# Rotary embedding: the first tile loaded in pieces of 1, 3 and 4 rows, tables behind the first row, and other rows and PSUM buffers

## The chip, the cores and the metric

One core of a Trainium2 chip. The experiments were spread over three chips: e1 to e4 and e9 to e12 ran on one, e5 to e8 on another, e13 to e15 on a third; every ratio is to runs of before in the same rounds on the same chip. The metric is device microseconds (us) of one execution; a kernel's time is the median of its fast runs. Beside it stands the span of the profiled execution, which is 1.8 to 1.9 us shorter.

## The reference

```python
batch, seq, dim = 16, 512, 1024          # float32, 16 heads of 64, half = 32
x = x.reshape(batch, seq, 16, 64)
x1, x2 = x[..., :32], x[..., 32:]        # cos, sin: (512, 32)
out = concatenate([x1*cos - x2*sin, x1*sin + x2*cos], axis=-1)
```

33.6 MB are read and 33.6 MB written; each element takes two products and a sum.

## The kernel before

The 16 x 512 positions are eight tiles (4 MiB each) of 128 partitions by eight rows of 1024 elements. A partition's eight rows lie together in HBM, so a tile is 128 runs of 32 KB. Five tiles have a buffer.

```python
BUFS = 5
PE_ROWS = (0, 2, 4, 6)
DVE_B = ((0,), (0, 4))
FIRST = (3, 8)                 # the first tile: rows 0-2, then 3-7
...
    pe = ctx.enter_context(tc.tile_pool(name="pe", bufs=2, space=bass.MemoryType.PSUM))
    pd = ctx.enter_context(tc.tile_pool(name="pd", bufs=1, space=bass.MemoryType.PSUM))
...
    load(0, 0, FIRST[0])                                  # all loads and stores: SyncE's queue
    for sb, v, parts in ((sin_sb, sin_v, SIN_PARTS), (cos_sb, cos_v, COS_PARTS)):
        ...  nc.sync.dma_start(out=sb[lo:hi, :], in_=v[lo:hi, :])
    for lo, hi in zip(FIRST, FIRST[1:]):
        load(0, lo, hi)
    for t in range(1, BUFS):
        load(t)
...  # the tables are spread to 128 partitions by two matmuls
    for t in range(NT):
        for k in range(KK):
            ...
            if not own:       # own: k in DVE_B[t % 2]
                nc.gpsimd.tensor_tensor(out=halves(b), in0=swapped(r, nh), in1=over_heads(sk), op=ALU.mult)
            if k in PE_ROWS:  # PSUM += by TensorE, ScalarE copies back
                ps = pe.tile([P, dim], FP32, name="ps")
                nc.vector.tensor_tensor(out=pairs(ps), in0=pairs(r), in1=cos_b(k), op=ALU.mult)
                ...           # two matmuls with the identity add the sine part
                nc.scalar.copy(out=r, in_=ps)
            else:             # VectorE adds, one row later
                nc.vector.tensor_tensor(out=pairs(ps), in0=pairs(r), in1=cos_b(k), op=ALU.mult)
                pending.append((r, ps, b))
        ...
        store(t)              # the last tile in two halves
        if t + 1 == NT - BUFS:
            for n in range(BUFS, NT):
                load(n)       # each waits for the store that frees its buffer
```

## Time and profile before

163.27 us (median of 3, 163.15 to 163.57), span 161.6 us.

| what | value | where |
|---|---|---|
| bytes moved, rate 3 to 158 us | 67.28 MB, 430 GB/s | page; windows of time |
| DMA queue's share of 16 engines' span | 97.5% | page, part 3 |
| VectorE, GpSimd busy | 128.9, 121.0 us | page, part 1 |
| VectorE's first row product, last add's end | 10.96, 142.96 us | timeline |
| least time from a store's issue to its landing | 17.5 us | view of out_dram |

Lines of the page of before. The second line is part 1. The DMA line gives the busy tenths of the DMA engines in 40 slices of the span, the GB/s line what they moved. The queue line is part 3, the next the chain of work that ended last, the last four the DMA issues with size and time from issue to landing.

```profile
span 161.6 us, 692 instructions
...
PE 81.8 (51%) x136; PEld 30.3 (19%) x136; DVE 128.9 (80%) x115; ACT 33.7 (21%) x33; POOL 121.0 (75%) x58
...
DMA  5999999999999999999999999999999999999992
GB/s 189 395 441 435 454 454 389 446 462 389 438 470 389 389 446 464 389 454 446 397 454 446 397 448 446 406 454 438 406 450 438 406 448 438 414 454 389 438 426 118
...
q1 hardware_dynamic: 2752, 67.24, 97.5%
...
DVE 37%; PE 18%; issue 17%; POOL 6%; ACT 4%; DMA 4%; SPq 0%; DVEq 0%; ACTq 0%; POOLq 0%
...
xt<-in_x_dram SPq DMA_DIRECT2D x1, 2560.0 KB, 11.3
xt<-in_x_dram SPq DMA_DIRECT2D x1, 1536.0 KB, 6.2
b<-in_sin_dram SPq DMA_DIRECT2D x1, 64.0 KB, 6.3
b<-in_cos_dram SPq DMA_DIRECT2D x1, 64.0 KB, 6.1
```

The DMA is full from the second slice to the last but one, so the bytes set the time. The chain of waits names VectorE first, yet it ends with the last store's issue at 143 us, and the transfers go on for 17 us more.

Windows of time of before: the last two columns are the DMA engines' busy share and GB/s. In such a window a DMA packet counts with all its bytes where it starts, so short windows are ragged.

```profile
3.00:4.00 1.00, 0.08 (x1) 0.00 (x0) 0.00 (x0) 0.00 (x0) 0.00 (x0) 1.00 0.99 418
4.00:5.00 1.00, 0.00 (x0) 0.00 (x0) 0.00 (x0) 0.00 (x0) 0.00 (x0) 1.00 1.00 418
5.00:6.00 1.00, 0.00 (x0) 0.00 (x0) 0.00 (x0) 0.00 (x0) 0.00 (x0) 1.00 0.96 406
...
143.00:158.00 15.00, 0.00 (x0) 0.00 (x0) 0.00 (x0) 0.00 (x0) 0.00 (x0) 0.58 0.98 422
```

The head flows at 406 to 418 GB/s; after 143 us, with all compute engines idle, the rate (422 GB/s) is close to the 430 of the whole stretch from 3 to 158 us.

SyncE's timeline of before: start and duration of each DMA issue (not of the transfer).

```profile
0.73 0.38 SPq L75 DMA_DIRECT2D xt<-in_x_dram  x1
1.17 0.53 SPq L87 DMA_DIRECT2D b<-in_sin_dram  x1
1.75 0.58 SPq L87 DMA_DIRECT2D b<-in_cos_dram  x1
2.37 2.65 SPq L75 DMA_DIRECT2D xt<-in_x_dram  x5
28.04 0.35 SPq L79 DMA_DIRECT2D out_dram<-xt  x1
```

### The profile page before, as it was taken

The page shows a single profiled execution, that of the slowest core. Times are in us where ns is not written, and L with a number is a line of the kernel's source. Part 1 is how long each engine was busy: PE and PEld are TensorE (multiplying, and loading weights), DVE is VectorE, ACT ScalarE, POOL GpSimd, SP SyncE. Part 2 cuts the span into 40 slices and gives each one's busy share as a digit, 9 for nine tenths or more (in the row PEclk, how much of TensorE's full clock was granted, in tenths as well). Part 3 has the DMA queues.
Part 4 walks back from the last instruction along what each step waited for, and adds up shares of the span by engine and source line. Part 5 has one row for each costly group of instructions (what it writes and reads, how often), then busy time and mean ns, then how long its engine had stood idle before and what let it go on. Part 6 is the DMA issues. An engine that isn't in the chain of part 4 may idle for free.

```text
span 161.6 us, 692 instructions
## 1 busy us (share of the span) xinstructions
PE 81.8 (51%) x136; PEld 30.3 (19%) x136; DVE 128.9 (80%) x115; ACT 33.7 (21%) x33; POOL 121.0 (75%) x58
## 2 busy tenths in 40 slices
PE   4136946496429742955097419660984194600000
PEld 1112301241114211311032114210321131100000
DVE  1059897999999989999999999999999999930000
ACT  0003242023302430223113302222223122220000
POOL 1049999999999999999994199999999997000000
PEclk9999996559975998799969965999689879995555
DMA  5999999999999999999999999999999999999992
GB/s 189 395 441 435 454 454 389 446 462 389 438 470 389 389 446 464 389 454 446 397 454 446 397 448 446 406 454 438 406 450 438 406 448 438 414 454 389 438 426 118
DMA packets 2756, 67.28 MB, mean 416 GB/s; under 512 B 320, under 2 KB 448, under 8 KB 448
## 3 DMA queue, kind: packets, MB, share of 16 engines
q1 hardware_dynamic: 2752, 67.24, 97.5%
q8 instruction: 1, 0.02, 0.0%
q14 instruction: 3, 0.02, 0.0%
HBM read 33.69 MB, written 33.55 MB: 416 GB/s over the span
## 4 chain that ended last, share of the span: by engine, by line
DVE 37%; PE 18%; issue 17%; POOL 6%; ACT 4%; DMA 4%; SPq 0%; DVEq 0%; ACTq 0%; POOLq 0%
PE ps L168 17%; DVE xt L150 12%; DVE pd L178 12%; DVE ps L163 7%; POOL b L160 6%; DVE xt L165 5%; ACT xt L171 4%; DMA b<-in_sin_dram 4%; PE tab L110 1%; PE tab L111 1%; DVE tab L118 0%; DVE sns L113 0%; SPq L75 0%; DVE sns L114 0%; DVEq L150 0%
## 5 line engine op out<-in xcount | busy, mean ns | idle before, releaser
L160 POOL TENSOR_TENSOR b<-xt,sns 128x1024 f32<-128x1024 f32 x52 | 120.3, 2350 | 14.5 <-DVE sns L114 9.2
L168 PE MATMUL ps<-xt,ident 128*128 128x512 f32 x48 | 35.8, 888 | 39.2 <-issue 24.5
L171 ACT COPY xt<-ps 128x1024 f32<-128x1024 f32 x32 | 32.4, 1012 | 95.2 <-PE ps L168 90.8
L168 PE MATMUL ps<-b,ident 128*128 128x512 f32 x80 | 43.5, 674 | 14.7 <-DVE ps L163 12.1
L150 DVE TENSOR_TENSOR xt<-pd,b 128x1024 f32<-128x1024 f32 x32 | 39.0, 1218 | 2.2 <-POOL b L160 1.1
L163 DVE TENSOR_TENSOR ps<-xt,tab 128x1024 f32<-128x1024 f32 x32 | 39.1, 1223 | 1.5 <-ACT xt L171 1.3
L178 DVE TENSOR_TENSOR pd<-xt,tab 128x1024 f32<-128x1024 f32 x32 | 39.3, 1227 | 0.8
L168 PEld LDWEIGHTS ps<-b,ident 128*128 128x128 f32 x80 | 17.1, 227 | 44.1 <-issue 30.6
L168 PEld LDWEIGHTS ps<-xt,ident 128*128 128x128 f32 x48 | 11.6, 267 | 58.8 <-issue 46.1
L165 DVE TENSOR_TENSOR xt<-xt,tab 128x1024 f32<-128x1024 f32 x12 | 14.6, 1220 | 0.4
L113 DVE TENSOR_SCALAR sns<-tab 128x256 f32<-128x256 f32 x1 | 0.4, 425 | 8.0 <-PE tab L111 8.0
L171 ACT ACT_TABLE_LOAD x1 | 1.3, 1283 | 13.5 <-DVE xt L165 13.5
L110 PE MATMUL tab<-b,spread 64*128 64x256 f32 x2 | 1.2, 697 | 4.5 <-DMA b<-in_sin_dram 4.5
L101 PE MATMUL ps<-zero 128*128 128x512 bf16 x4 | 1.9, 625 | 1.2 <-DVE zero L97 1.2
L110 PEld LDWEIGHTS tab<-b,spread 64*128 64x128 f32 x2 | 0.5, 308 | 5.4 <-issue 5.4
L111 PE MATMUL tab<-b,spread 64*128 64x256 f32 x2 | 1.1, 631 | 0.0
L97 DVE MEMSET zero<- 128x256 uint32 x1 | 0.3, 272 | 0.9 <-PEq L208 0.9
L101 PEld LDWEIGHTS <-zero 128*128 128x128 bf16 x4 | 0.4, 129 | 1.7 <-DVE zero L97 1.2
L111 PEld LDWEIGHTS tab<-b,spread 64*128 64x128 f32 x2 | 0.7, 333 | 0.2
L118 DVE COPY tab<-sns 128x64 f32<-128x64 f32 x2 | 0.5, 228 | 0.1
L109 DVE COPY spread<-ident 64x64 f32<-64x64 f32 x2 | 0.3, 182 | 0.2 <-POOL ident masks.py:199 0.2
masks.py:197 POOL MEMSET ident<- 128x128 f32 x1 | 0.2, 204 | 0.3 <-POOLq L208 0.3
(6 smaller groups left out, 1.1 us busy)
## 6 DMA issues: line engine op xcount, KB each, us to landing
xt<-in_x_dram SPq DMA_DIRECT2D x7, 4096.0 KB, 29.5
out_dram<-xt SPq DMA_DIRECT2D x7, 4096.0 KB, 30.3
out_dram<-xt SPq DMA_DIRECT2D x2, 2048.0 KB, 18.1
xt<-in_x_dram SPq DMA_DIRECT2D x1, 2560.0 KB, 11.3
xt<-in_x_dram SPq DMA_DIRECT2D x1, 1536.0 KB, 6.2
b<-in_sin_dram SPq DMA_DIRECT2D x1, 64.0 KB, 6.3
b<-in_cos_dram SPq DMA_DIRECT2D x1, 64.0 KB, 6.1
```

What stands on the lines that cost most here:

```text
L101: nc.tensor.matmul(out=ps[:, c : c + BANK], lhsT=zero[:, :P], rhs=zero, start=True, stop=True)
L110: nc.tensor.matmul(out=sin_t, lhsT=spread, rhs=sin_sb, start=True, stop=True)
L111: nc.tensor.matmul(out=cos_t, lhsT=spread, rhs=cos_sb, start=True, stop=True)
L113: nc.vector.tensor_scalar_mul(out=sns[:, :, 0, :], in0=sin_k, scalar1=-1.0)
L118: nc.vector.tensor_copy(out=sns_t[:, i * hd : (i + 1) * hd], in_=sns[:, k])
L150: nc.vector.tensor_tensor(out=r, in0=ps, in1=b, op=ALU.add)
L160: nc.gpsimd.tensor_tensor(out=halves(b), in0=swapped(r, nh), in1=over_heads(sk), op=ALU.mult)
L163: nc.vector.tensor_tensor(out=pairs(ps), in0=pairs(r), in1=cos_b(k), op=ALU.mult)
L165: nc.vector.tensor_tensor(out=halves(r), in0=halves(r), in1=swapped_signed(k), op=ALU.mult)
L168: nc.tensor.matmul(out=ps[:, c : c + BANK], lhsT=ident, rhs=rhs, start=False, stop=True, skip_group_check=True)
L171: nc.scalar.copy(out=r, in_=ps)
L178: nc.vector.tensor_tensor(out=pairs(ps), in0=pairs(r), in1=cos_b(k), op=ALU.mult)
```

## The change

Its intent: start the compute earlier (one row and the tables suffice), let TensorE, ScalarE and VectorE wait less for PSUM (three single-bank buffers and two of two banks in place of two and one of two banks), and keep adds one row behind. The core of the diff:

```diff
-PE_ROWS = (0, 2, 4, 6)
-DVE_B = ((0,), (0, 4))
-FIRST = (3, 8)
+PE_ROWS = (0, 3, 6)
+DVE_B = ((0,), (0,))
+FIRST = (1, 4, 8)
...
-    pe = ...(name="pe", bufs=2, ...)      # tiles of 1024 (two banks)
-    pd = ...(name="pd", bufs=1, ...)
+    pe = ...(name="pe", bufs=3, ...)      # tiles of 512 (one bank)
+    pd = ...(name="pd", bufs=2, ...)
...
-                ps = pe.tile([P, dim], FP32, name="ps")
-                nc.vector.tensor_tensor(out=pairs(ps), in0=pairs(r), in1=cos_b(k), op=ALU.mult)
+                for c in range(0, dim, BANK):
+                    ps = pe.tile([P, BANK], FP32, name="ps")
+                    nc.vector.tensor_tensor(out=pairs(ps), in0=pairs(rc), in1=cos_b(k, BANK // half), op=ALU.mult)
...   # matmul and ScalarE's copy also by halves; at most one add pending
+            if k == 0 and t > 0:
+                finish(t - 1)             # last add and store of the tile before
```

More of the change, by code (lines that the diff above doesn't have):

```diff
@@ L16 @@
 BANK = 512
-PE_ROWS = (0, 2, 4, 6)
-DVE_B = ((0,), (0, 4))
-FIRST = (3, 8)
+PE_ROWS = (0, 3, 6)
+DVE_B = ((0,), (0,))
+FIRST = (1, 4, 8)
 LAST_OUT = (4, 8)
-SIN_PARTS = (64,)
-COS_PARTS = (64,)
 @with_exitstack
@@ L63 @@
     pfix = ctx.enter_context(tc.tile_pool(name="pfix", bufs=1, space=bass.MemoryType.PSUM))
-    pe = ctx.enter_context(tc.tile_pool(name="pe", bufs=2, space=bass.MemoryType.PSUM))
-    pd = ctx.enter_context(tc.tile_pool(name="pd", bufs=1, space=bass.MemoryType.PSUM))
+    pe = ctx.enter_context(tc.tile_pool(name="pe", bufs=3, space=bass.MemoryType.PSUM))
+    pd = ctx.enter_context(tc.tile_pool(name="pd", bufs=2, space=bass.MemoryType.PSUM))
     ctx.enter_context(tc.manual_schedule())
@@ L83 @@
     cos_sb = bp.tile([P, dim], FP32, name="b")[:PB, : KK * half]
-    for sb, v, parts in ((sin_sb, sin_v, SIN_PARTS), (cos_sb, cos_v, COS_PARTS)):
-        lo = 0
-        for hi in parts:
-            nc.sync.dma_start(out=sb[lo:hi, :], in_=v[lo:hi, :])
-            lo = hi
+    nc.sync.dma_start(out=sin_sb, in_=sin_v)
+    nc.sync.dma_start(out=cos_sb, in_=cos_v)
     for lo, hi in zip(FIRST, FIRST[1:]):
@@ L97 @@
     nc.vector.memset(zero, 0.0)
-    for i in range(2):
-        ps = pe.tile([P, dim], FP32, name="ps")
-        for c in range(0, dim, BANK):
-            nc.tensor.matmul(out=ps[:, c : c + BANK], lhsT=zero[:, :P], rhs=zero, start=True, stop=True)
+    for i in range(3):
+        ps = pe.tile([P, BANK], FP32, name="ps")
+        nc.tensor.matmul(out=ps, lhsT=zero[:, :P], rhs=zero, start=True, stop=True)
     sns = fixed.tile([P, KK, 2, half], FP32)
@@ L118, with cos_b @@
         nc.vector.tensor_copy(out=sns_t[:, i * hd : (i + 1) * hd], in_=sns[:, k])
-    def cos_b(k):
+    def cos_b(k, n):
         c = cos_t[:, k * half : (k + 1) * half]
-        return bass.AP(tensor=c.tensor, offset=c.offset, ap=[c.ap[0], [0, 2 * nh], [1, half]])
+        return bass.AP(tensor=c.tensor, offset=c.offset, ap=[c.ap[0], [0, n], [1, half]])
     def over_heads(s):
@@ L146, with add, finish @@
     pending = []
-    def add():
-        r, ps, b = pending.pop(0)
-        nc.vector.tensor_tensor(out=r, in0=ps, in1=b, op=ALU.add)
+    def add(most):
+        while len(pending) > most:
+            r, ps, b = pending.pop(0)
+            nc.vector.tensor_tensor(out=r, in0=ps, in1=b, op=ALU.add)
+    def finish(t):
+        add(0)
+        lo = 0
+        for hi in LAST_OUT if t == NT - 1 else (KK,):
+            store(t, lo, hi)
+            lo = hi
+        if t + 1 == NT - BUFS:
+            for n in range(BUFS, NT):
+                load(n)
     for t in range(NT):
@@ L161 @@
             if k in PE_ROWS:
-                ps = pe.tile([P, dim], FP32, name="ps")
-                nc.vector.tensor_tensor(out=pairs(ps), in0=pairs(r), in1=cos_b(k), op=ALU.mult)
+                parts = []
+                for c in range(0, dim, BANK):
+                    ps = pe.tile([P, BANK], FP32, name="ps")
+                    rc = r[:, c : c + BANK]
+                    nc.vector.tensor_tensor(
+                        out=pairs(ps), in0=pairs(rc), in1=cos_b(k, BANK // half), op=ALU.mult
+                    )
+                    parts.append((ps, rc, swapped(rc, BANK // hd) if own else b[:, c : c + BANK]))
                 if own:
                     nc.vector.tensor_tensor(out=halves(r), in0=halves(r), in1=swapped_signed(k), op=ALU.mult)
-                for c in range(0, dim, BANK):
-                    rhs = swapped(r[:, c : c + BANK], BANK // hd) if own else b[:, c : c + BANK]
-                    nc.tensor.matmul(
-                        out=ps[:, c : c + BANK], lhsT=ident, rhs=rhs, start=False, stop=True, skip_group_check=True
-                    )
-                nc.scalar.copy(out=r, in_=ps)
-                while pending:
-                    add()
-            else:
-                while pending:
-                    add()
+                for ps, rc, rhs in parts:
+                    nc.tensor.matmul(out=ps, lhsT=ident, rhs=rhs, start=False, stop=True, skip_group_check=True)
+                    nc.scalar.copy(out=rc, in_=ps)
+            else:
+                add(1)
                 ps = pd.tile([P, dim], FP32, name="pd")
-                nc.vector.tensor_tensor(out=pairs(ps), in0=pairs(r), in1=cos_b(k), op=ALU.mult)
+                nc.vector.tensor_tensor(out=pairs(ps), in0=pairs(r), in1=cos_b(k, 2 * nh), op=ALU.mult)
                 pending.append((r, ps, b))
-        while pending:
-            add()
-        if t < NT - 1:
-            store(t)
-        else:
-            lo = 0
-            for hi in LAST_OUT:
-                store(t, lo, hi)
-                lo = hi
-        if t + 1 == NT - BUFS:
-            for n in range(BUFS, NT):
-                load(n)
+            if k == 0 and t > 0:
+                finish(t - 1)
+            add(1)
+    finish(NT - 1)
 _INS = ['x', 'cos', 'sin', 'num_heads']
```

## The prediction

> **What bounds the kernel now: the DMA engines.** The page counts 67.28 MB moved and a DMA strip that reads 9 in every slice from the second to the last but one. By windows of time, 3 to 158 us moved 430 GB/s at a DMA share of 1.00. The Trainium skill, "DMA: Bandwidth & Descriptors", section "Specifications", puts the fabric ceiling at 435 GB/s; this trace agrees. The rate does not depend on the compute: 143 to 158 us, with every compute engine idle, moved 422 GB/s.
>
> The chain of waits names DVE 37% and PE 18%, but it ends at 142.96 us, when the last store is issued; that lands 17.5 us later (least issue-to-landing among stores). So compute runs well ahead. The second half of the last store (2.1 MB, about 4.9 us at 430 GB/s) can first move at about 154 us: some 11 us to spare.
>
> **What the change does.**
> - *Head.* 0.5 MB instead of 1.57 MB lies before the tables, so they land about 2.5 us earlier (1.05 MB at 418 GB/s): near 5 us, not 7.43; DVE's first row product starts near 8.4 us, not 10.96. But the same 20 MB of loads queue, and the first store waits behind them (issued 28.04, loads run to about 52).  Cost: one more DMA and 128 packets; perhaps 0 to 0.3 us of bubble while the short first piece drains.
> - *DVE.* Rows through PE go from 32 to 24, so 8 more rows take a second DVE pass (add, 1.218 us); rows with DVE's own product go from 12 to 8 (1.220 us each saved); 24 products split into 48 of 512. From 1.222 us for 1024 and 0.24 us for 64 elements I estimate 0.69 us a half. Sum about +8 us: DVE busy near 138 us, not 128.9.
> - *POOL.* 56 instead of 52 products at 2.35 us: about 131 us, +9.
> - *ACT* 48 copies of 512 (about 0.55 us each, estimate): about 26 us. *PE*: 96 recorded main matmuls instead of 128.
> - *PSUM.* Three single banks for PE rows and two pairs for DVE rows, adds deferred by one: fewer waits between DVE, ACT and POOL. Stores are issued one row later, about 3 us. All off the critical path.
>
> Compute should end at 145 to 152 us (8.4 + 138 + a few us of waits), still before the queue runs dry at about 154. The DMA then finishes where it did.
>
> **Predicted: 163.3 us**, 162.6 to 164.4 holding 8 times in 10. Chances: faster by over 2%: 0.02; within 2%: 0.94; slower by over 2%: 0.04. The Trainium skill, "Perfetto Trace Analysis", section "DMA Optimizations", says splitting DMAs may pay when the engines are generally idle; here they are not.
>
> **What would show each step.** Right: DMA strip still at 9, about 430 GB/s in the middle, span within 1 us of 161.6; DVE starts near 8.4 us, is busy near 138 us, ends 145 to 152; POOL about 131 us; last store's issue to landing falls to about 10 us, yet time stays. Wrong: a hole in the DMA strip near 3 us or after 140 us, or a different rate with equal bytes.
>
> **What would make it wrong.** Compute ending after about 153 us (slow clock stretching PE, POOL late), each us then costing one; a lower DMA rate from the smaller head pieces or another overlap of loads and stores; or a start bubble over 0.3 us.

## The result, and the profile after

| | before | after |
|---|---|---|
| time, median of 6 runs each | 163.32 us (163.13 to 163.57) | 164.97 us (164.42 to 165.42) |
| ratio of fast runs | | 1.0098 (1.0077 to 1.0120) |
| span of the profiled run | 161.6 us | 163.0 us |

A ratio here is the mean time of one kernel's fast runs over that of the other's fast runs of the same rounds, so it is not quite the ratio of the medians. The outputs are right. The change is about 1% slower: within the 2% that counts as the same, but clear of noise and outside the predicted range.

The lines of the page of after that answer to those of before:

```profile
span 163.0 us, 616 instructions
...
PE 78.3 (48%) x103; PEld 24.8 (15%) x103; DVE 131.8 (81%) x142; ACT 29.4 (18%) x49; POOL 130.2 (80%) x62
...
DMA  5999999999999999999999999999999899999992
GB/s 153 348 435 470 418 442 442 402 450 450 418 442 306 452 434 426 450 410 442 442 410 442 450 396 466 426 434 442 410 434 466 386 442 458 410 450 394 438 418 92
...
q1 hardware_dynamic: 2896, 67.24, 97.2%
...
DVE 8%; issue 1%; DVEq 1%
...
xt<-in_x_dram SPq DMA_DIRECT2D x1, 2048.0 KB, 11.8
xt<-in_x_dram SPq DMA_DIRECT2D x1, 1536.0 KB, 7.6
xt<-in_x_dram SPq DMA_DIRECT2D x1, 512.0 KB, 3.9
b<-in_sin_dram SPq DMA_DIRECT2D x1, 64.0 KB, 3.6
b<-in_cos_dram SPq DMA_DIRECT2D x1, 64.0 KB, 3.9
```

(The chain of waits of after covers only a tenth of the span, so nothing is read from it.) The compute started earlier, as meant: the first product at 8.07 us, not 10.96. It still ended later, at 144.03 us and not 142.96, with more work on VectorE. And the same bytes took longer. The GB/s line shows where: the first two slices fell from 189 and 395 to 153 and 348, and the thirteenth (49 to 53 us) to 306. The busy digits hide both, because a packet that takes long counts as busy all along, and a few tenths of a us without a packet (below) are less than a tenth of a slice of 4.1 us.

Windows of time of after:

```profile
3.00:4.00 1.00, 0.00 (x0) 0.00 (x0) 0.00 (x0) 0.00 (x0) 0.00 (x0) 1.00 0.85 329
4.00:5.00 1.00, 0.06 (x1) 0.09 (x1) 0.00 (x0) 0.30 (x1) 0.00 (x0) 1.00 1.18 220
5.00:6.00 1.00, 1.00 (x3) 0.67 (x4) 0.00 (x0) 0.98 (x1) 0.00 (x0) 1.00 0.87 348
...
144.10:158.00 13.90, 0.00 (x0) 0.00 (x0) 0.00 (x0) 0.00 (x0) 0.00 (x0) 0.55 0.99 424
```

Between 4 and 5 us 220 GB/s are booked in place of 418, at a busy share over 1: few packets start there, and those that do take long. The tail is unchanged.

SyncE's timeline of after:

```profile
0.73 0.38 SPq L72 DMA_DIRECT2D xt<-in_x_dram  x1
1.17 0.53 SPq L81 DMA_DIRECT2D b<-in_sin_dram  x1
1.74 0.58 SPq L82 DMA_DIRECT2D b<-in_cos_dram  x1
2.37 3.32 SPq L72 DMA_DIRECT2D xt<-in_x_dram  x6
29.93 0.35 SPq L76 DMA_DIRECT2D out_dram<-xt  x1
```

The issues stand at the same times, but the first now carries a third of the bytes. One row's packets occupy the engines from 1.74 to 4.04 us, cold start included, against 6.42 for three rows.

The trace also records each DMA packet (one run of one partition) with start, duration and bytes, and the moment at which each of the 16 engines reports the end of its share of a DMA. From these, in us:

```
                                              before   after
first packet starts                             1.74    1.74
packets of the 2nd piece: first 16, median      1.038   1.044   (20 KB; 12 KB)
  the same piece, median of all                 0.766   0.460
tile 0 landed, median engine (last engine)     13.39 (13.64)   14.08 (14.82)
tile 3 landed, median engine                   42.51   43.23
tile 4 landed, median engine (last engine)     52.50 (52.80)   53.64 (55.17)
last store landed, median (last engine)       159.13 (160.50) 160.41 (161.81)
slow packets of 32 KB between 36 and 60 us:
  time over 1.213 us, sum per engine            0.36    0.94
time without a packet, 3.0 to 6.5 us, per engine  0.00    0.29
```

(The row of slow packets takes those of over 1.230 us, sums what each took beyond 1.213 us, the usual time, and divides by 16 engines. The last row counts the packets under way at each moment; where they are fewer than 16, the missing ones are summed over time and divided by 16.)

The last row is the direct sign of a queue that has run dry. It is 0.22 to 0.58 us in all seven traces with one row ahead of the tables on SyncE's queue (after 0.29, its second trace 0.58, e1 0.58, e4 0.53, e7 0.38, e8 0.22, e9 0.57), and at most 0.02 us in the ten others, e3, e5 and e6 among them. (e7, e13 and e14 run dry on purpose later, near 13 to 17 us.)

Two losses, then. By the median engine, 0.69 us are lost in the first tile, and 0.44 more between the landings of tiles 3 and 4 (10.42 us against 9.98), where the DMA turns from loads to the first store: some 30 of the last load packets, about two for each engine, take 1.3 to 2.4 us where 1.213 is usual. Nothing is won back. In a second trace of each kernel (below) the two terms were 0.88 and 0.46.

### The profile page after: what moved, and what is told of

The parts are those of the page before. It is cut to its first block, busy times and chain, and to the rows that moved or that the text cites. A ratio compares the mean times of both kernels' runs of the same rounds, so it can differ in the third digit from the quotient of the medians.

```text
span 163.0 us, 616 instructions
## 1 busy us (share of the span) xinstructions
PE 78.3 (48%) x103; PEld 24.8 (15%) x103; DVE 131.8 (81%) x142; ACT 29.4 (18%) x49; POOL 130.2 (80%) x62
## 5 line engine op out<-in xcount | busy, mean ns | idle before, releaser
L164 POOL TENSOR_TENSOR b<-xt,sns 128x1024 f32<-128x1024 f32 x56 | 129.5, 2368 | 11.6 <-DMA xt<-in_x_dram 11.6
L177 PE MATMUL ps<-b,ident 128*128 128x512 f32 x64 | 50.5, 935 | 42.1 <-POOL b L164 26.4
L144 DVE TENSOR_TENSOR xt<-pd,b 128x1024 f32<-128x1024 f32 x40 | 48.6, 1218 | 0.7 <-POOL b L164 0.7
L182 DVE TENSOR_TENSOR pd<-xt,tab 128x1024 f32<-128x1024 f32 x40 | 48.2, 1223 | 0.3
L178 ACT COPY xt<-ps 128x512 f32<-128x512 f32 x48 | 28.1, 585 | 108.7 <-PE ps L177 108.7
L170 DVE TENSOR_TENSOR ps<-xt,tab 128x512 f32<-128x512 f32 x48 | 30.9, 688 | 4.3 <-DMA xt<-in_x_dram 2.8
L177 PE MATMUL ps<-xt,ident 128*128 128x512 f32 x32 | 24.3, 902 | 18.3 <-DVE xt L175 7.8
L177 PEld LDWEIGHTS ps<-b,ident 128*128 128x128 f32 x64 | 15.5, 267 | 75.8 <-POOL b L164 56.4
L177 PEld LDWEIGHTS ps<-xt,ident 128*128 128x128 f32 x32 | 7.9, 274 | 35.8 <-issue 24.6
L175 DVE TENSOR_TENSOR xt<-xt,tab 128x1024 f32<-128x1024 f32 x8 | 9.8, 1222 | 0.4
```

The costliest lines, as they stand in the source:

```text
L144: nc.vector.tensor_tensor(out=r, in0=ps, in1=b, op=ALU.add)
L170: nc.vector.tensor_tensor(out=pairs(ps), in0=pairs(rc), in1=cos_b(k, BANK // half), op=ALU.mult)
L175: nc.vector.tensor_tensor(out=halves(r), in0=halves(r), in1=swapped_signed(k), op=ALU.mult)
L177: nc.tensor.matmul(out=ps, lhsT=ident, rhs=rhs, start=False, stop=True, skip_group_check=True)
L178: nc.scalar.copy(out=rc, in_=ps)
```

## The experiments

Theory H: the short first piece and two slow table issues let the DMA queue run dry, or nearly so, before the second big piece; that time is lost for good. Rival R: the new split of rows and PSUM buffers makes compute and DMA collide. Rivals S and T: small packets or more pieces cost time in themselves.

All outputs were right. "Head" is the landing of the first tile on the median engine; "turn" is the slow packets' excess per engine, as above; both are from the one profiled execution. A single execution's state is called unknown, so single runs are used for their traces alone. The medians of before beside them were 163.22 to 163.37 us.

| run | time | ratio to before | head | turn |
|---|---|---|---|---|
| before | 163.32 | | 13.39 | 0.36 |
| after | 164.97 | 1.0098 | 14.08 | 0.94 |
| e1_head_alone | 165.21 | 1.0107 | 13.88 | 0.98 |
| e2_old_head | 163.26 | 0.9990 | 13.42 | 0.39 |
| e3_tables_third | 163.68 | 1.0007 | 13.37 | 0.36 |
| e4_two_pieces | 164.74 | 1.0079 | 13.87 | 0.89 |
| e5_tables_on_act | 162.90 | 0.9972 | 13.56 | 0.06 |
| e6_two_rows | 163.57 | 1.0002 | 13.31 | 0.72 |
| e7_wait_after_first | 168.00 | 1.0281 | 14.05 | 1.14 |
| e8_turn_earlier | 165.41 | 1.0114 | 13.87 | 1.36 |
| e9_touch_output | 165.59 | 1.0150 | 14.13 | 0.66 |
| e10_after_again | one run | | 14.30 | 0.82 |
| e11_before_again | one run | | 13.42 | 0.36 |
| e12_act_again | one run | | 13.57 | 0.16 |
| e13_old_head_wait | one run | | 13.38 | 1.01 |
| e14_act_wait | one run | | 13.65 | 0.94 |
| e15_before_act | 163.09 | 0.9992 | 13.48 | 0.13 |

### e1_head_alone: the new head on the kernel before

```diff
-FIRST = (3, 8)            # in the kernel before
+FIRST = (1, 4, 8)
```

> The kernel before with one line changed: the first tile in pieces of 1, 3 and 4 rows, tables behind the first row; its rows, PSUM buffers and order of compute stay. Theory H (the short first piece runs the DMA queue dry before the second big piece has started, and the time lost there is never won back): slower than before by 1.2 to 1.8 us, ratio 1.007 to 1.011; the DMA strip or fine windows show a dip near 4 to 5.5 us; DVE starts near 7 us, about 4 us earlier, for nothing. Rival R (the new row split and PSUM buffers change how compute and DMA collide, above all in the slow packets near 50 to 53 us): ratio 0.999 to 1.002, with at most 0.3 us lost.

Measured: 165.21 us (164.94 to 165.51), ratio 1.0107 (1.0081 to 1.0133). The one line makes the whole loss, without any of the compute change. R is refuted. The dip is there too: the engines were without a packet for 0.58 us each between 3.0 and 6.5 us.

### e2_old_head: the changed kernel with the old head

```diff
-FIRST = (1, 4, 8)         # in the changed kernel
+FIRST = (3, 8)
```

> The changed kernel with the old head (3 rows, tables, 5 rows); all of the compute change stays. Theory H: the time of before, ratio 0.998 to 1.002, although DVE works about as long as in the changed kernel and ends about 3 to 4 us later than there. Rival R: the changed kernel's time, ratio 1.008 to 1.011.

Measured: 163.26 us, ratio 0.9990 (0.9965 to 1.0015). The loss is gone with all of the compute change still there. One detail missed: VectorE ended at 142.4 us, not 3 to 4 us later than in the changed kernel (144.0); its waits for loads fell from 2.8 to 0.4 us, which is part of the reason.

### e3_tables_third: the same three pieces, tables behind the second

```diff
     load(0, 0, FIRST[0])
+    load(0, FIRST[0], FIRST[1])
     nc.sync.dma_start(out=sin_sb, in_=sin_v)
     nc.sync.dma_start(out=cos_sb, in_=cos_v)
-    for lo, hi in zip(FIRST, FIRST[1:]):
+    for lo, hi in zip(FIRST[1:], FIRST[2:]):
```

> The changed kernel with the same three pieces of 1, 3 and 4 rows, but the tables issued behind the second piece, so 1.5 MB is queued back to back before the small table packets. Theory H (dry queue): the queue never empties, ratio 0.998 to 1.003, no dip near 4 to 5.5 us. Rival S (small packets and one more DMA cost time in themselves, wherever they stand): ratio 1.007 to 1.011 as for the changed kernel.

Measured: 163.68 us, ratio 1.0007 (0.9982 to 1.0033), with as many DMAs and the same packets as the changed kernel. Small packets and the number of pieces (S) cost nothing that can be seen. Windows of time of this run:

```profile
3.00:4.00 1.00, 0.00 (x0) 0.00 (x0) 0.00 (x0) 0.00 (x0) 0.00 (x0) 1.00 1.16 479
4.00:5.00 1.00, 0.00 (x0) 0.00 (x0) 0.00 (x0) 0.72 (x1) 0.00 (x0) 1.00 1.02 418
5.00:6.00 1.00, 0.00 (x0) 0.00 (x0) 0.00 (x0) 0.56 (x1) 0.00 (x0) 1.00 1.05 442
```

No dip. The first 16 packets of the second piece took 0.460 us (median), the same as the later ones, where the changed kernel's took 1.044. So here the second piece was already under way when the first ended. The third piece, behind the tables, still began a little slow (0.769 us against 0.615).

### e4_two_pieces: 1 and 7 rows

```diff
-FIRST = (1, 4, 8)
+FIRST = (1, 8)
```

> The changed kernel with the first tile in two pieces of 1 and 7 rows, tables between them: as many DMAs as before. Theory H: the dip is before the second piece whatever its size, so the full loss stays, ratio 1.006 to 1.011. Rival S (number of pieces): at most half of the loss, ratio below 1.005. Compute starts only when the 7 rows have landed near 14 us and should end near 150 us, still before the last store can move.

Measured: 164.74 us, ratio 1.0079 (1.0051 to 1.0106). As many DMAs as before and still most of the loss: it is the gap ahead of the second piece, not a third piece. VectorE ended at 146.6 us, earlier than expected.

### e5_tables_on_act: the tables issued from ScalarE's queue

```diff
-    nc.sync.dma_start(out=sin_sb, in_=sin_v)
-    nc.sync.dma_start(out=cos_sb, in_=cos_v)
+    nc.scalar.dma_start(out=sin_sb, in_=sin_v)
+    nc.scalar.dma_start(out=cos_sb, in_=cos_v)
```

> The changed kernel with the two table loads issued from ScalarE's queue instead of SyncE's, so the three pieces of the first tile are issued back to back (second piece at about 1.2 us instead of 2.4). The tables still reach the DMA engines beside the first row. Theory H (the queue runs dry because the second piece is issued too late, behind two table issues of 0.53 and 0.58 us): the loss is gone, ratio 0.995 to 1.002, and the engines' landings of the first tile lie within 0.4 us of each other. Rival T (the small table packets so early stall the engines in themselves): loss stays, ratio above 1.005.

Measured: 162.90 us (162.69 to 163.30), ratio 0.9972 (0.9948 to 0.9996). SyncE's timeline of this run: all seven loads of x now follow one another.

```profile
0.73 4.48 SPq L72 DMA_DIRECT2D xt<-in_x_dram  x7
```

Windows of time of this run:

```profile
3.00:4.00 1.00, 0.00 (x0) 0.00 (x0) 0.00 (x0) 0.00 (x0) 0.00 (x0) 1.00 1.27 461
4.00:5.00 1.00, 0.00 (x0) 0.03 (x1) 0.00 (x0) 0.30 (x1) 0.00 (x0) 1.00 0.88 338
5.00:6.00 1.00, 1.00 (x2) 0.47 (x2) 0.00 (x0) 0.98 (x1) 0.00 (x0) 1.00 1.08 421
```

The three windows are uneven, but their mean is 407 GB/s, against 299 in the changed kernel and 414 in before, and the engines were without a packet for only 0.01 us. The short first piece costs no time once the next is issued right behind it, though the sine table's packets run beside it (landed at 4.87 us). T falls, for that table. One part was missed: the landings of the first tile spread over 0.64 us (13.21 to 13.85), not 0.4. The cosine table landed later than in the changed kernel (8.94 us, not 5.69), beside the second piece, so VectorE's first product came at 11.30 us; the time did not mind.

### e6_two_rows: 2, 2 and 4 rows

```diff
-FIRST = (1, 4, 8)
+FIRST = (2, 4, 8)
```

> The changed kernel with first pieces of 2, 2 and 4 rows, tables behind the first two rows. Theory H: two rows are about 2.4 us of transfer, the second piece is ready before they end, so the queue does not run dry: ratio 0.999 to 1.004. A rival that the loss grows smoothly with the shortness of the first piece (3 rows 0, 1 row 1.6 us) says about 0.8 us, ratio 1.005.

Measured: 163.57 us, ratio 1.0002 (0.9973 to 1.0030). Two rows nearly cover the table issues: the head is not late on the median engine (13.31), though the last engine is (14.23 against 13.64 before). So the loss in time does not grow smoothly with the shortness of the piece. But the turn cost 0.72, within what the kernels that ran dry show, though in this trace no engine was without a packet in the head (0.00 us between 3.0 and 6.5 us); one engine was only late.

### e7_wait_after_first, e13_old_head_wait, e14_act_wait: a dry moment on purpose

The same edit in the changed kernel (e7), in e2 (e13) and in e5 (e14):

```diff
+    mark = fixed.tile([P, 8], FP32)
+    nc.sync.dma_start(out=mark, in_=tiles[0][:, F - 8 :])   # waits for the whole first tile
     for t in range(1, BUFS):
         load(t)
```

> The changed kernel with a copy of eight elements per partition, from the last piece of the first tile to a scratch tile, issued before the loads of tiles 1 to 4: SyncE waits there until the first tile has landed on all engines, so all engines start the next loads together, later by some 2 us. Theory D (the slow packets at the end of the fifth load cost more where the engines have drifted apart): the spread of the landings of tile 1 falls from 1.1 to below 0.5 us and the extra time of the slow packets falls from 0.94 us per engine to about 0.4. Rival L (it is lateness alone, or what is queued, that makes them slow): it stays near 0.9 or grows. Total: 165.5 to 167.5 us either way.

Measured: 168.00 us (two runs), ratio 1.0281. The total was above its range. The spread of tile 1's landings fell to 0.51 us, near what was expected, but the turn rose to 1.14. Theory D, that drift between engines makes the slow packets, falls. Rival L, lateness, had allowed such a rise and stands. So the last round asked whether any dry moment does.

> The changed kernel's compute with the old head (3 rows, tables, 5 rows) and the wait of e7 behind the first tile. Its queue never ran dry inside the first tile, but runs dry once at 13.7 us. Theory Q (a queue that has run dry once, wherever, pays more at the first turn to stores): slow packets cost 0.8 to 1.2 us per engine, as in e7. Rival: what counts is the head itself (a short first piece), then 0.3 to 0.5 as in the kernel with the old head without the wait.

> The variant with the tables on ScalarE's queue and the same wait behind the first tile. Theory Q: the cost of the slow packets at the first turn rises from 0.06 and 0.16 to 0.8 or more. Rival: it stays below 0.3.

Measured: one run each, spans 164.8 and 165.1 us. The turn rose from 0.39 to 1.01 and from 0.06 and 0.16 to 0.94. A kernel whose queue had not run dry gets the large cost some 40 us later as soon as it is made to wait once, with the old head too. Theory Q's forecast held. But the edit does more than dry the queue: it adds a small copy, and tile 3 landed 3.1 us later than in e2 (45.65 for 42.56 us) and 3.5 us later than in e5 (46.20 for 42.71). So these runs do not tell a dry moment from mere lateness, and the copy was not tried without the wait.

### e8_turn_earlier: the load of tile 4 behind the first store

```diff
-    for t in range(1, BUFS):
+    for t in range(1, BUFS - 1):
         load(t)
...
     def finish(t):
         ...
+        if t == 0:
+            load(BUFS - 1)
```

> The changed kernel with the load of tile 4 issued behind the first store, so that the DMA goes from loads to stores one tile sooner, near 43 us, and back again. If the slow packets belong to the first turn from loads to stores, they lie near 40 to 45 us, and the load of tile 4 runs at full rate. If they belong to tile 4 (its addresses) or to a moment of the run near 50 us, they stay there or at tile 4 (54 to 64 us). The time is expected within 0.5% of the changed kernel.

Measured: 165.41 us (164.18 to 166.10), ratio 1.0114 (1.0073 to 1.0155). The slow packets moved to 40 to 44 us, and tile 4 then came at full rate (9.57 us behind the first store on the median engine; a load took 9.71 between the turns). They belong to the first turn from loads to stores. At the later turn, near 110 us, they cost at most 0.19 us per engine in any trace.

### e9_touch_output: a small store to the output first

```diff
+    nc.sync.dma_start(out=out_v[0][:, :8], in_=ident[:, :8])   # the first store overwrites it
     for t in range(1, BUFS):
         load(t)
```

> The changed kernel with one small store of eight elements per partition into the first tile's place in the output, issued behind the first tile's loads (the real first store overwrites it, and waits for it). Theory F (the slow packets at the first turn from loads to stores come of the output being written for the first time): they vanish or fall below 0.4 us per engine, and the time falls to 163.9 to 164.4. Rival: they stay at 0.7 to 1.1 us and the time at 164.7 to 165.5.

Measured: 165.59 us (165.56 to 165.90), ratio 1.0150; the turn cost 0.66. Theory F, a cold output, is not supported: the excess fell a little but stayed far above the 0.36 of before. Turn and time lie just outside the rival's ranges as well (0.7, and 165.5 us), and the small store cost more than it saved.

### e10_after_again, e11_before_again, e12_act_again: second traces

Nothing was edited.

> The changed kernel again, unaltered, for a second trace. If the two losses are the kernel's own, the first tile lands again at 14.1 to 14.4 us (median engine) and the slow packets at the first turn cost again 0.8 to 1.1 us per engine; if the second is chance, it will differ by more than 0.3 us.

> The kernel before again, unaltered, for a second trace: the first tile lands at 13.6 to 13.7 us, and the slow packets cost 0.3 to 0.45 us per engine if they are the kernel's own.

> The variant with the tables on ScalarE's queue again, for a second trace: the first tile lands near 13.8 us; if the small loss at the first turn (0.06 us per engine) was its own, it stays below 0.2, if it was chance it is 0.3 to 0.4 as in the kernel before.

Measured: heads 14.30, 13.42 and 13.57 us, turns 0.82, 0.36 and 0.16 (spans 163.5, 161.5 and 161.4). Both losses are the kernels' own, not chance. The heads of the last two came earlier than the 13.6 to 13.7 and 13.8 us expected.

### e15_before_act: tables on ScalarE's queue in the kernel before

```diff
-            nc.sync.dma_start(out=sb[lo:hi, :], in_=v[lo:hi, :])
+            nc.scalar.dma_start(out=sb[lo:hi, :], in_=v[lo:hi, :])
```

> The kernel before with nothing changed but the two table loads, issued from ScalarE's queue; rows, PSUM buffers and the pieces of 3 and 5 rows stay. If the gain of e5 over the kernel before (ratio 0.9972) comes of the queue alone and not of the new compute, this one is as fast: 0.995 to 0.999. If it needs the new compute, 1.000.

Measured: 163.09 us (162.90 to 163.24), ratio 0.9992 (0.9978 to 1.0005). The turn fell from 0.36 to 0.13, and the first packets of the second piece were no longer slow (0.791 us against 0.800 of the piece; before 1.038 against 0.766). The time is not clearly better. Whether e5's 0.3% needs its compute as well stays open.

## Why the prediction was right or wrong

- **"What bounds the kernel now: the DMA engines": right.** The compute change alone moved nothing (e2, 0.9990), and a later or earlier end of compute (142.4 us in e2, 146.6 in e4) did not set the time. Splitting did not pay; the section "DMA Optimizations" of "Perfetto Trace Analysis" in the Trainium skill holds out a gain where DMA engines are generally idle, and here they are not.
- **The failed step: "perhaps 0 to 0.3 us of bubble while the short first piece drains".** The sign was right, the size was not: the median engine lost 0.69 us (0.88 in the second trace) by the end of the first tile. The prediction named "a start bubble over 0.3 us" among what would make it wrong, but gave no working for its 0 to 0.3. The packets show the bubble: each engine was without a packet for 0.29 us (0.58 in the second trace) between 3.0 and 6.5 us, where before has none; slow packets make the rest. What was left out is how late the second piece is issued, at 2.37 us, and how long its first packets then take: 1.044 us (median) in place of 0.460, and 0.744 in the second trace. A rough estimate from the trace: 2.37, plus 1.01 from an issue to its first packet, plus about 1.04 for a first packet, is 4.4 us, and the first piece was through at 4.04. In e3 the same sum gives about 3.2 us (issued at 1.16), and the first piece ended at 3.85: no gap. With the 0.744 of the second trace the sum is 4.1 us against 4.05, so it says that there is no margin, and not how much is lost. e1, e2, e3 and e5 show the cause. A smaller part is not the short piece's: big packets right behind the tables start slow in before too (1.038 us against 0.766), and no longer with the tables on the other queue (e15).
- **"The DMA then finishes where it did": wrong also by a term that the prediction did not size.** It named "another overlap of loads and stores" as a danger, no more. At the first turn from loads to stores 0.44 us more were lost (0.46 in the second trace). That goes largely with a dry moment: the slow packets cost 0.06 to 0.39 us per engine in seven traces without one (before, e2, e3, e5, e11, e12, e15) and 0.66 to 1.36 in the nine with one (after, e1, e4, e7, e8, e9, e10, e13, e14). But e6 cost 0.72 without one. Lateness sorts the traces as well, e6 too: where the last engine had landed tile 3 by 43.17 us, the turn cost at most 0.39; where it landed it at 43.37 us or later, at least 0.66 (e8 left out, which turns a tile earlier). The cost does not grow with lateness: 0.98 in e1, whose median engine was 0.5 us late at tile 3, and 1.01 in e13, 3.1 us late. e13 and e14 brought a dry moment and lateness together, so which of the two is the cause is not shown, nor what in the machine carries it over some 40 us; drift of the engines (e7) and a cold output (e9) did not explain it.
- **The sum.** Median engine: 0.69 + 0.44 = 1.13 us at tile 4, and 1.28 at the last store. Last engine: 1.31. Spans: 1.45; timed medians: 1.65. In the second traces: 0.88 + 0.46 = 1.34, and 1.81 on the last engine. The remaining difference between these measures (drift of the last engine, and single executions) was not taken apart.
- **Compute.** Tables and first product came as predicted (8.07 us for 8.4), and so did GpSimd (130.2 for 131). VectorE was over-estimated: busy 131.8 us, not 138. The step that failed there was to add durations to a busy time: one by one its products and adds do sum to 8.4 us more (140.5 for 132.1), close to the +8 forecast, but consecutive instructions overlap and busy time counts an overlap once, so it rose by 2.9 only (the 48 half products last 0.688 us each, 33.0 in sum, and are busy for 30.9). It ended at 144.03, just below the range, so the last store's issue to landing stayed at 17.7 us where about 10 was predicted. That the end of compute fell near its range is partly luck, since the busy time was 6 us too high. None of it set the time.

## What to carry to other kernels

When the DMA is the bound, look at the queue before the compute: a short piece ahead of several issues can leave the engines dry, because the next bulk must be issued early enough for its slow first packets to be under way when the piece ends. Count the packets under way to see it: the busy strip did not show it. Issue the bulk back to back and put small loads behind it or on another engine's queue, and let the compute start later if it has slack. A queue that ran dry or late may cost again later, so compare landing times along the whole run and not just where the change is.

## What the Trainium skill lacked or had wrong

- "DMA: Bandwidth & Descriptors", section "Issuing engines are not separate DMA queues", says that issuing from several engines only saves the sequencer's issue time, "which is usually small relative to the DMA itself". Here two table issues of 0.53 and 0.58 us stood before the second piece, and taking them off that queue took the changed kernel from 1.0098 to 0.9972 of before.
- "Perfetto Trace Analysis", section "DMA Optimizations", says that splitting may help when engines are generally idle; it lacks the cost when they are not. With two table issues behind it on the same queue, a first piece of one row cost 1% (1.0107 in e1), one of two rows nothing (1.0002 in e6).
- No page tells of the slow load packets at the first turn from loads to stores: 0.06 to 0.39 us per engine in seven traces, 0.66 to 1.36 in the ten whose queue ran dry or whose last engine was late.
- The Trainium skill's "DMA: Bandwidth & Descriptors", section "Specifications", gives about 0.6 us to the first byte for DMAs issued from SyncE, and does not say from when. In these traces the first packet starts 1.01 us after its issue began (0.73 to 1.74) and 0.63 us after the issue ended (1.11), so the figure agrees if it is counted from the end. The page lacks that the first packets behind a gap then run slow (1.044 us in place of 0.460 in after).
